# Hybrid encoder layer on one core: gate rows, token rows and Toeplitz blocks issued at other places

## The chip, the cores and the metric

The kernel runs on one core of a Trainium2 chip. Its time is device microseconds (us) from start to end of one execution. TensorE is called PE (its weight loads PEld), VectorE DVE, ScalarE ACT, GpSimd POOL and SyncE SP. SP issues most transfers between the chip's memory (DRAM) and on-chip memory, each by one instruction of its queue. POOL and ACT issue some too.

## What is computed

One layer (`DEPTH = 1`) of a hybrid encoder, in fp32, on a prompt of 2048 rows and 64 sample rows that continue a cached stream of 2048:

```
h = rms(x, ln1);  q, k, v, fg, u, hc, gb, gc = split(h @ w_in)     # 8 heads of 64
logf = log_sigmoid(fg + bf);  c = cumsum(logf)
s = q k^T / 8 + c_q - c_k, causal;  att = softmax(s) v
y_ssm, state = s5(u)            # 16 groups of 16 channels, 64 complex states each
ssm = gelu(y_ssm) * sigmoid(gelu(y_ssm) @ w_glu + b_glu)
conv = gb * shortconv(gc * hc)
x = x + concat(rms(att), rms(ssm), rms(conv)) @ w_out
x = x + relu(rms(x) @ w_up)^2 @ w_down
```

The outputs are the new rows, keys, values, gate logs, S5 states and conv states of both streams.

## The kernel before

`phase1` (to about 542 us) makes the in-projection and leaves queries and keys (`qk_d`), values (`v_d`), token rows of the S5 branch (`u_d`) and gate sums (`nc_d`) in DRAM; its last part is the conv. `attention` (to about 1080 us) goes over the eight prompt heads. Out-projection, up-projection and down-projection follow and are not touched.

For a head `h`, `load(h)` (L1196) brings into one of two sets of tiles: `kb` (keys with three gate rows from `nc_d`, 24 KB, L1200, and 64 key rows, 512 KB, L1201), `q1` (64 transposed query rows, L1202; its three last rows carry maxima, for head 0 from `m_d` by ACT, L1207) and `ka` (keys again, two halves, L1203 and L1204). `load_v` (L1210) brings the values, 1 MB, into `v3`, and `load_q2` (L1215) one block of 512 transposed queries, two transfers of 128 KB (L1220, L1221). In the trace `q1` and `q2` are both called `q`, `v3` is `v`. `scores` runs units of a head in the order of `order()`: two products into `st` (L1239 reads `kb` and `q1`, L1240 `ka` and `q2`), the exponential on ACT (L1248), its split into `ph` and `pl`, and the products with `v` into `po` (L1260, L1262, L1267). Beside them `row_max` (L1149, L1154) takes the maxima of the next head, for which that head's `kb` and `q1` must be there.

Between units `fill(w)` advances a chain of generators by weights that they `yield`: `s5_branch` (L786), in which a `yield -1` hands over to `sample_attention` for four pairs of sample heads, then w_out and the output of the sample rows. `s5_branch` loads its token rows in three chunks of 704 KB (`s5ut`, `load_u`, L808), the first at its start, makes tables, writes kernels to `kp_d`, and loads these as eight Toeplitz blocks of 256 KB (`s5mt`, L922), which `s5py` reads from 944 us on. `sample_attention` loads 512 cached keys at a time (`sa_y`, L1084), transposes them in four products (`sa_pk`, L1081) and makes scores (`sa_ps`, L1090, L1091); a chunk's load overwrites what the transposes before it read.

A scheduler writes each engine's order from the order of the code and its priorities; each engine runs its own order in sequence. A transfer of SP or ACT signals its landing on one of eight semaphores in turn, so it also waits for the transfer eight before it. POOL stores the conv state (L419, L423) and the S5 states (L952) in pieces of four bytes.

Of the kernel before, what the change touches and what calls it, by code (L numbers as in the profile page):

```python
# [48 lines left out]
def f32(ap):  # L49
    return ap.bitcast(F32)  # L50
# [735 lines left out]
def s5_branch(g, pool, sp):  # L786

    nc, I, O = g.nc, g.I, g.O
# [129 lines left out]
        nc.sync.dma_start(hs[hh, 129, :], I[src][0, 0].rearrange("g p -> p g"))  # L918

    mt = pool.tile([128, G, 256], F32, tag="gm", name="s5mt")  # L920
    for t in range(8):
        nc.sync.dma_start(mt[16 * t:16 * t + 16],  # L922
                          g.kp_d[:, :, 16 * (7 - t):16 * (7 - t) + 256].rearrange("g c n -> c g n"))
        yield 1
    r1 = sp.tile([128, 16, G], F32, tag="yg", bufs=3, name="s5r1")
    r2 = sp.tile([128, 16, G], F32, tag="yg", bufs=3, name="s5r2")

# [240 lines left out]
def attention(ctx, g, fill):  # L1168

    tc, nc = g.tc, g.nc  # L1170
# [7 lines left out]
    ka, kb, q1, v3 = [], [], [], []  # L1178
# [17 lines left out]
    def load(h):  # L1196
        i, hp, e = h % 2, h // 2, h % 2
        r = slice(64 * e, 64 * e + 64)
        qk = g.qk_d[hp]
        nc.sync.dma_start(f32(kb[i])[64:67, :], g.nc_d[:, h, :])  # L1200
        nc.sync.dma_start(f32(kb[i])[0:64, :], qk[0, 1, r, :])  # L1201
        nc.sync.dma_start(f32(q1[i])[0:64, :], qk[0, 0, r, :])  # L1202
        nc.sync.dma_start(f32(ka[i])[0:64, :], qk[0, 1, r, :])  # L1203
        nc.sync.dma_start(f32(ka[i])[64:128, :], qk[1, 1, r, :])  # L1204
        if h == 0:
            load_q2(0, 3)
            nc.scalar.dma_start(f32(q1[i])[64:67, :], g.m_d)  # L1207
            load_v(0)

    def load_v(h):  # L1210
        i, hp, e = h % 2, h // 2, h % 2
        nc.sync.dma_start(f32(v3[i])[:, :, 0:128],
                          g.v_d[hp][e])

    def load_q2(h, sb):  # L1215
        hp, e = h // 2, h % 2
        r = slice(64 * e, 64 * e + 64)
        c = slice(sb * 512, sb * 512 + 512)
        t = pp.tile([128, 512], F32R, tag="q2", bufs=3, name=f"q2{h}_{sb}")
        nc.sync.dma_start(f32(t)[0:64, :], g.qk_d[hp][1, 0, r, c])  # L1220
        nc.sync.dma_start(f32(t)[64:128, :], g.qk_d[hp][0, 0, r, c])  # L1221
        q2[h, sb] = t
# [59 lines left out]
    def order():  # L1282
        full = {sb: [(sb, (k, k + 1)) for k in range(0, 4 * sb, 2)] for sb in range(4)}
        diag = {sb: [(sb, (4 * sb,)), (sb, (4 * sb + 1,)), (sb, (4 * sb + 2, 4 * sb + 3))] for sb in range(4)}
        f3, f2, f1 = full[3], full[2], full[1]
        d3, d2, d1, d0 = diag[3], diag[2], diag[1], diag[0]
        u = f3[:2] + [d3[0], f3[2], d0[0], f3[3], d3[1], d0[1], f3[4], d0[2], f3[5], d3[2]]
        u += f2[:2] + [d2[0], f1[0], d1[0], f2[2], d2[1], f1[1], d1[1], f2[3], d1[2], d2[2]]
        seen, out = {}, []
        left = {sb: len(full[sb]) + 3 for sb in range(4)}  # L1290
        for sb, b in u:
            left[sb] -= 1
            w = 2.2 if b[0] < 4 * sb else 1.2
            out.append((sb, b, sb not in seen, left[sb] == 0, w))
            seen[sb] = 1
        return out

    units = order()
    total = sum(u[4] for u in units)
    fill(0.1)  # L1300
    load(0)
    pend, pend2 = [], []

    def late(n, m):
# [8 lines left out]
    for h in range(H):  # L1313
# [9 lines left out]
        for n, (sb, batch, first, last, w) in enumerate(units):  # L1323
            if n == 0 and h + 1 < H:
                load(h + 1)
            if n == 1:
                load_q2(h, 0)
            if n == 3 and h + 1 < H:
                load_v(h + 1)
            if n == 6:  # L1330
                load_q2(h, 2)
            if n == 11:
                load_q2(h, 1)
            if n == len(units) - 4 and h + 1 < H:
                load_q2(h + 1, 3)
            pend.append(scores(h, sb, batch, first, last))
            if n >= 2:
                owed += 43.0 * w / (total * 0.74)
            maxima()
            if len(pend) > 2:  # L1340
                f, f2 = pend.pop(0)
                f()
                pend2.append(f2)
            maxima()
            fill(w)
            if len(pend2) > 1:
                pend2.pop(0)()
            maxima()
            g.late = h + 1 == H and n >= 12
# [12 lines left out]
def w_out_tiles(g, pool, tags, dtype, out):  # L1362
    for tag, n in tags:
        t = pool.tile([128, n, D], dtype, tag=tag, name=f"wo_{tag}{len(out)}")
        out += [t[:, j, :] for j in range(n)]


def w_out_load(g, pool, tags):
    k0 = len(g.wo_r)
    w_out_tiles(g, pool, tags, F32, g.wo_r)  # L1370
    for k in range(k0, len(g.wo_r)):
        g.nc.sync.dma_start(g.wo_r[k], g.I["w_out"][0, k * 128:k * 128 + 128, :])


def w_out_split(g, k):

    nc = g.nc
    raw, hi, lo, w = g.wo_r[k], g.wo_h[k], g.wo_l[k], g.bn[:, k:k + 1]
    nc.scalar.activation(hi, raw, AF.Copy, scale=w)
    nc.vector.scalar_tensor_tensor(lo, raw, w, f32(hi), op0=ALU.mult, op1=ALU.subtract)  # L1380
# [474 lines left out]
@with_exitstack  # L1855
def hybrid_step_kernel(ctx, tc, I, O, dbg=None):
    g = setup(ctx, tc, I, O)
    with ExitStack() as c1:
        phase1(c1, g)
    with ExitStack() as c2:  # L1860
        fpool = c2.enter_context(tc.tile_pool(name="fill", bufs=1, side="right", reuse_waits="tile"))
        fsp = c2.enter_context(tc.tile_pool(name="fills", bufs=1, side="right", reuse_waits="tile"))

        def chain():
            for y in s5_branch(g, fpool, fsp):
                if y < 0:
                    yield from sample_attention(g, fpool, fsp, (0, 1))
                    g.idle = True
                    yield from sample_attention(g, fpool, fsp, (2, 3))
                else:  # L1870
                    yield y

            w_out_load(g, fpool, (("hs", 2), ("ych", 2)))
            w_out_tiles(g, fpool, (("u", 4),), F32R, g.wo_h)
            w_out_tiles(g, fpool, (("x1", 2), ("x2", 2)), F32R, g.wo_l)
            yield 4
            for k in range(4, 8):
                w_out_split(g, k)
                yield 0
            yield from out_sample(g, fpool)  # L1880
            while not g.late:
                yield 0
            g.prep[0] = out_prep(g, 0)
            for _ in range(3):
                next(g.prep[0])
                yield 4

        clock = Ctx()
        clock.now, clock.ready, clock.budget = 0.0, 0.0, 0.0
        it = chain()  # L1890

        def side_by_side(*gens):
            ready = {x: clock.now for x in gens}
            while ready:
                x = min(ready, key=ready.get)
                if ready[x] > clock.now:
                    yield ready[x] - clock.now
                y = next(x, None)
                if y is None:
                    del ready[x]  # L1900
                else:
                    ready[x] = clock.now + y
                    if y == 0:
                        yield 0

        g.side_by_side = side_by_side

        def fill(w):

            clock.now += w * 1.68  # L1910
            clock.budget = min(clock.budget + w, 4.0)
            while clock.budget > 0 and clock.now >= clock.ready:
                y = next(it, None)
                if y is None:
                    break
                clock.ready = max(clock.now + y, clock.ready)
                clock.budget -= 0.4 if y > 0 else 1.25

        g.ah = c2.enter_context(tc.tile_pool(name="ah", bufs=1, reuse_waits="tile"))
        g.os = c2.enter_context(tc.tile_pool(name="os", bufs=2, reuse_waits="tile"))  # L1920
        g.ready, g.prep, g.late, g.idle = {}, {}, False, False
        g.fpool, g.fsp = fpool, fsp
        with ExitStack() as c2a:
            attention(c2a, g, fill)
            for _ in it:
                pass
        with ExitStack() as c3:
            phase3a(c3, g)
    g.wts, g.fts, g.first = {}, {}, {}
    with ExitStack() as c6:  # L1930
        g.xp = c6.enter_context(tc.tile_pool(name="both", bufs=1, reuse_waits="tile"))
        with ExitStack() as c4:
            phase_up(c4, g)
        with ExitStack() as c5:
            phase_down(c5, g)
    if dbg is not None:
        dbg(g)
# [30 lines left out]
```

## Time and profile before

| | |
|---|---|
| time, median of 3 runs | 2792.05 us (2791.56 to 2795.51) |
| the profiled execution's own time | 2794.95 us |
| its span, first to last instruction | 2793.2 us |
| granted TensorE clock, mean | 0.979 |
| busy share of PE, DVE, ACT, POOL | 97%, 60%, 44%, 15% |

The profile is of one execution, and its times are from the start of the span. The granted clock is the share of full speed (2.4 GHz) that PE was given; 0.50 is the lower level, 1.2 GHz. An engine's idle time is put down to what ended it, as inferred from semaphores; "issue" is a time for which the profile shows no releaser.

### The profile page before, as it was taken

Reading aid. Unit: us, or ns where it says so; the run is one execution under the profiler, and the core shown is the slowest. Engines: PE = TensorE matmul, PEld = TensorE weight load, DVE = VectorE, ACT = ScalarE, POOL = GpSimd, SP = SyncE. Lnnn points to the kernel's source line nnn. Section 1 sums busy time; section 2 is a strip of 40 time slices with the busy share of each in tenths; the row PEclk is TensorE's granted clock in tenths of the full one; section 3 lists DMA queues with packets and bytes.
Section 4 is the critical chain, followed back from the end, with each engine's and each line's share of the span. In section 5 each row is a group of like instructions: output and inputs, shape, how many; then the busy total and the mean of one; then the engine's idle time right before and its main releaser. Section 6 shows DMA issues by size and latency. Waiting matters only on the chain.

```text
span 2793.2 us, 38960 instructions
## 1 busy us (share of the span) xinstructions
PE 2699.9 (97%) x14438; PEld 2341.8 (84%) x14438; DVE 1681.7 (60%) x3375; ACT 1230.3 (44%) x2383; POOL 415.4 (15%) x566
## 2 busy tenths in 40 slices
PE   7999999888899999899989999999999999999999
PEld 7999998755567776688789999999998888888887
DVE  7637468477575576577786686686644344434433
ACT  5424243156577677833265676576641111111110
POOL 2101105123752224432300000000000000000000
PEclk9999999989899999999999999999999999999999
DMA  7636546643644223375545353344354122212123
GB/s 216 186 109 185 165 104 177 111 99 93 108 100 109 72 71 89 116 213 165 177 137 176 131 176 127 133 156 136 128 198 151 51 78 80 78 48 78 49 79 117
DMA packets 358929, 347.13 MB, mean 124 GB/s; under 512 B 43726, under 2 KB 316446, under 8 KB 354734
## 3 DMA queue, kind: packets, MB, share of 16 engines
q1 hardware_dynamic: 356189, 336.87, 41.8%
q0 software_dynamic: 2240, 7.01, 0.8%
q8 instruction: 114, 1.87, 0.3%
q14 instruction: 76, 0.62, 0.1%
q10 hardware_dynamic: 310, 0.75, 0.1%
HBM read 237.05 MB, written 107.46 MB: 123 GB/s over the span
## 4 chain that ended last, share of the span: by engine, by line
PE 85%; DMA 4%; issue 4%; DVE 3%; ACT 2%; POOL 1%; SPq 1%; ACTq 0%; DVEq 0%; POOLq 0%
PE pa L1641 12%; PE pd L107 8%; PE pd L108 8%; PE pd L106 8%; PE pd L1641 6%; PE pb L1641 3%; PE pq L106 3%; PE pq L108 3%; PE pq L107 3%; PE mx L1149 2%; PE po L106 2%; PE st L1239 2%; PE po L107 2%; PE po L108 2%; PE st L1240 2%
## 5 line engine op out<-in xcount | busy, mean ns | idle before, releaser
L1820 DVE TENSOR_TENSOR acc<-acc,pd 128x512 f32<-128x512 f32 x272 | 186.7, 686 | 411.2 <-PE pd L108 406.0
L106 PE MATMUL pd<-dw,fh 128*128 128x512 f32 x1016 | 395.2, 389 | 0.0
L108 PE MATMUL pd<-dw,fl 128*128 128x512 f32 x1016 | 395.2, 389 | 0.0
L107 PE MATMUL pd<-dw,fh 128*128 128x512 f32 x1016 | 395.2, 389 | 0.0
L1789 ACT ACTIVATE fh<-fr 128x512 fp32r<-128x512 f32 x127 | 80.2, 632 | 530.9 <-PE pd L107 520.9
L1252 DVE TENSOR_TENSOR pl<-p,ph 128x512 fp32r<-128x512 f32 (+2 forms) x246 | 171.5, 715 | 110.7 <-ACT ph L1251 104.5
L107 PEld LDWEIGHTS pd<-dw,fh 128*128 128x128 f32 x1016 | 190.7, 188 | 39.7
L108 PEld LDWEIGHTS pd<-dw,fl 128*128 128x128 f32 x1016 | 190.7, 188 | 39.6
L106 PEld LDWEIGHTS pd<-dw,fh 128*128 128x128 f32 x1016 | 190.7, 188 | 39.5
L1154 DVE TENSOR_REDUCE pm<-mx 128x1 f32<-128x512 f32 (+2 forms) x320 | 184.3, 607 | 58.7 <-PE mx L1153 32.3
L1248 ACT ACTIVATE p<-st 128x512 f32<-128x512 f32 (+2 forms) x320 | 164.3, 544 | 89.8 <-PE st L1240 34.2
L1641 PE MATMUL pa<-as,wt 128*128 128x352 f32 x1152 | 201.3, 323 | 0.8 <-ACT sm L1656 0.8
L1641 PEld LDWEIGHTS pa<-as,wt 128*128 128x128 f32 x1152 | 187.3, 188 | 2.0 <-ACT sm L1656 1.3
L106 PE MATMUL pq<-wh,xh 128*128 128x384 f32 (+1 forms) x512 | 179.4, 350 | 5.2 <-ACT xh L233 4.7
L1251 ACT ACTIVATE ph<-p 128x512 fp32r<-128x512 f32 (+2 forms) x320 | 173.8, 581 | 3.9 <-PE po L1262 1.8
L108 PE MATMUL pq<-wh,xl 128*128 128x384 f32 (+1 forms) x512 | 174.5, 341 | 0.5 <-DVE xl L234 0.3
L107 PE MATMUL pq<-wl,xh 128*128 128x384 f32 (+1 forms) x512 | 174.1, 340 | 0.0
L1586 DVE TENSOR_TENSOR wt<-tt,wt 128x512 fp32r<-128x512 f32 x192 | 131.4, 687 | 69.1 <-ACT wt L1585 65.9
L1586 DVE TENSOR_TENSOR w<-wr,w 128x512 fp32r<-128x512 f32 x144 | 99.0, 688 | 87.2 <-ACT w L1585 86.9
L1585 ACT ACTIVATE wt<-tt 128x512 fp32r<-128x512 f32 x192 | 120.4, 627 | 67.2 <-PE pd L1641 66.2
L1240 PE MATMUL st<-q,ka 128*128 128x512 f32 (+2 forms) x320 | 124.4, 393 | 12.0 <-DMA q<-qk_d 12.0
L1149 PE MATMUL mx<-kb,q 66*128 66x512 f32 (+2 forms) x280 | 113.4, 438 | 18.1 <-DVE pm L1154 11.1
(508 smaller groups left out, 6118.6 us busy)
## 6 DMA issues: line engine op xcount, KB each, us to landing
wr<-in_w_up_dram SPq DMA_DIRECT2D x46, 1024.0 KB
f_d<-sm SPq DMA_DIRECT2D x47, 704.0 KB
fr<-f_d SPq DMA_DIRECT2D x128, 256.0 KB
raw<-in_w_in_dram SPq DMA_DIRECT2D x51, 512.0 KB
dr<-in_w_down_dram SPq DMA_DIRECT2D x32, 512.0 KB
qk_d<-stgT SPq DMA_DIRECT2D x16, 768.0 KB
xt<-in_x_prompt_dram SPq DMA_DIRECT2D x16, 512.0 KB
ka<-qk_d SPq DMA_DIRECT2D x16, 512.0 KB
```

Of the source, the lines that this page charges most:

```text
L106: nc.tensor.matmul(out, lh, rh, start=first, stop=False)
L107: nc.tensor.matmul(out, lh, rl, start=False, stop=False)
L108: nc.tensor.matmul(out, ll, rh, start=False, stop=last)
L1149: nc.tensor.matmul(p[:, :n], q1[0:66, t * 128:t * 128 + 128], kb[0:66, k0 * 128:k0 * 128 + n], start=True, stop=not last)
L1154: nc.vector.tensor_reduce(pm[:, t, c:c + 1], p[:, :n], axis=AX.X, op=ALU.max)
L1240: nc.tensor.matmul(st[:, c0:], ka[i][:, kc], q2[h, sb][:, c0:512], start=False, stop=r < 0)
L1248: nc.scalar.activation(p[:, c0:], st[:, c0:], AF.Exp)
L1251: nc.scalar.activation(ph[:, c0:], p[:, c0:], AF.Copy)
L1252: (nc.gpsimd if g.idle and j else nc.vector).tensor_tensor(pl[:, c0:], p[:, c0:], f32(ph)[:, c0:], op=ALU.subtract)
L1586: ve.tensor_tensor(t[:, 1], x, f32(t)[:, 0], op=ALU.subtract)):
L1641: nc.tensor.matmul(bank, w[:, x, k], a[:, y, k], start=first and k + j == 0, stop=k + j == 5, skip_group_check=not first)
L1820: nc.vector.tensor_tensor(a[:, o], a[:, o], p, op=ALU.add)
```

## The change

In the first head, the gate rows are issued behind the first block of transposed queries, ahead of the values. `load(0)` stands ahead of `fill(0.1)`, so the first chunk of token rows is issued behind head 0's loads. The eight Toeplitz loads are taken out of `s5_branch`'s sequence into a generator, which runs side by side with the last two pairs of sample heads.

```
--- before.py
+++ after.py
@@ -918,10 +918,14 @@
         nc.sync.dma_start(hs[hh, 129, :], I[src][0, 0].rearrange("g p -> p g"))
 
     mt = pool.tile([128, G, 256], F32, tag="gm", name="s5mt")
-    for t in range(8):
-        nc.sync.dma_start(mt[16 * t:16 * t + 16],
-                          g.kp_d[:, :, 16 * (7 - t):16 * (7 - t) + 256].rearrange("g c n -> c g n"))
-        yield 1
+
+    def toeplitz():
+        for t in range(8):
+            yield 4
+            nc.sync.dma_start(mt[16 * t:16 * t + 16],
+                              g.kp_d[:, :, 16 * (7 - t):16 * (7 - t) + 256].rearrange("g c n -> c g n"))
+
+    g.toeplitz = toeplitz
     r1 = sp.tile([128, 16, G], F32, tag="yg", bufs=3, name="s5r1")
     r2 = sp.tile([128, 16, G], F32, tag="yg", bufs=3, name="s5r2")
 
@@ -1197,13 +1201,15 @@
         i, hp, e = h % 2, h // 2, h % 2
         r = slice(64 * e, 64 * e + 64)
         qk = g.qk_d[hp]
-        nc.sync.dma_start(f32(kb[i])[64:67, :], g.nc_d[:, h, :])
+        if h:
+            nc.sync.dma_start(f32(kb[i])[64:67, :], g.nc_d[:, h, :])
         nc.sync.dma_start(f32(kb[i])[0:64, :], qk[0, 1, r, :])
         nc.sync.dma_start(f32(q1[i])[0:64, :], qk[0, 0, r, :])
         nc.sync.dma_start(f32(ka[i])[0:64, :], qk[0, 1, r, :])
         nc.sync.dma_start(f32(ka[i])[64:128, :], qk[1, 1, r, :])
         if h == 0:
             load_q2(0, 3)
+            nc.sync.dma_start(f32(kb[i])[64:67, :], g.nc_d[:, h, :])
             nc.scalar.dma_start(f32(q1[i])[64:67, :], g.m_d)
             load_v(0)
 
@@ -1297,8 +1303,8 @@
 
     units = order()
     total = sum(u[4] for u in units)
+    load(0)
     fill(0.1)
-    load(0)
     pend, pend2 = [], []
 
     def late(n, m):
@@ -1866,7 +1872,7 @@
                 if y < 0:
                     yield from sample_attention(g, fpool, fsp, (0, 1))
                     g.idle = True
-                    yield from sample_attention(g, fpool, fsp, (2, 3))
+                    yield from side_by_side(sample_attention(g, fpool, fsp, (2, 3)), g.toeplitz())
                 else:
                     yield y
```

In the order of the engines the line numbers of the changed kernel are 3 to 6 higher. SP at the first head before; `kb_6570`, `q_6571`, `ka_6572`, `v_6573` are head 0's tiles, `kb_6577` and `q_6578` head 1's, `q_3` is `q2` of block 3:

```order
L1200 DMA kb_6570<-nc_d 3x2048
L1201 DMA kb_6570<-qk_d_60 64x2048
L808 DMA s5ut_6586<-u_d 88x2048
L1202 DMA q_6571<-qk_d_60 64x2048
L1203 DMA ka_6572<-qk_d_60 64x2048
L1204 DMA ka_6572<-qk_d_60 64x2048
L1220 DMA q_3_6593<-qk_d_60 64x512
L1221 DMA q_3_6593<-qk_d_60 64x512
L1212 DMA v_6573<-v_d_64 128x16x128
L1200 DMA kb_6577<-nc_d 3x2048
L1201 DMA kb_6577<-qk_d_60 64x2048
```

And in the changed kernel:

```order
L1206 DMA kb_6570<-qk_d_60 64x2048
L1207 DMA q_6571<-qk_d_60 64x2048
L1208 DMA ka_6572<-qk_d_60 64x2048
L1209 DMA ka_6572<-qk_d_60 64x2048
L1226 DMA q_3_6585<-qk_d_60 64x512
L1227 DMA q_3_6585<-qk_d_60 64x512
L1212 DMA kb_6570<-nc_d 3x2048
L1218 DMA v_6573<-v_d_64 128x16x128
L808 DMA s5ut_6596<-u_d 88x2048
L1205 DMA kb_6577<-nc_d 3x2048
L1206 DMA kb_6577<-qk_d_60 64x2048
```

The gate rows (`nc_d`) and `s5ut` have left the front; the gate rows stand ahead of `v`, `s5ut` behind it and ahead of head 1's loads. SP at the passage from head 2 to head 3 before; here `kb_6577`, `q_6578` and `ka_6575` are head 3's, `q_0` is `q2` of head 2, block 0:

```order
L922 DMA s5mt<-kp_d 16x16x256 x2
L1164 DMA q_6571<-mt_8117 1x16x128
L922 DMA s5mt<-kp_d 16x16x256 x4
L1200 DMA kb_6577<-nc_d 3x2048
L1201 DMA kb_6577<-qk_d_61 64x2048
L1202 DMA q_6578<-qk_d_61 64x2048
L1203 DMA ka_6575<-qk_d_61 64x2048
L1204 DMA ka_6575<-qk_d_61 64x2048
L922 DMA s5mt<-kp_d 16x16x256
L1220 DMA q_0_8243<-qk_d_61 64x512
L1221 DMA q_0_8243<-qk_d_61 64x512
```

And in the changed kernel:

```order
L1168 DMA q_6571<-mt_8311 1x16x128
L1081 DMA sa_c_8358<-ncs_d 4x1x512
L1088 DMA sa_y_8244<-in_cache_k_dram 128x4x128
L1205 DMA kb_6577<-nc_d 3x2048
L1081 DMA sa_c_8421<-ncs_d 4x1x512
L1088 DMA sa_y_8244<-in_cache_k_dram 128x4x128
L1206 DMA kb_6577<-qk_d_61 64x2048
L1207 DMA q_6578<-qk_d_61 64x2048
L1208 DMA ka_6575<-qk_d_61 64x2048
L1209 DMA ka_6575<-qk_d_61 64x2048
L1226 DMA q_0_8465<-qk_d_61 64x512
L1227 DMA q_0_8465<-qk_d_61 64x512
```

Six of the eight `s5mt` are no longer there (two are ahead of this piece, the others are issued beside later sample loads), and loads of sample keys (`sa_y`) and gate sums (`sa_c`) stand among head 3's loads. PE at the first units of head 2 before:

```order
L1239 MATMUL st_3_0_8218<-q_6571,kb_6570 128x512
L1240 MATMUL st_3_0_8218<-q_3_8120,ka_6572 128x512
L1239 MATMUL st_3_1_8225<-q_6571,kb_6570 128x512
L1240 MATMUL st_3_1_8225<-q_3_8120,ka_6572 128x512
L1239 MATMUL st_3_2_8246<-q_6571,kb_6570 128x512
L1240 MATMUL st_3_2_8246<-q_3_8120,ka_6572 128x512
L1239 MATMUL st_3_3_8253<-q_6571,kb_6570 128x512
L1240 MATMUL st_3_3_8253<-q_3_8120,ka_6572 128x512
```

And in the changed kernel:

```order
L1094 MATMUL sa_ps_8390<-sa_y_8244,qbd 128x512
L1245 MATMUL st_3_0_8436<-q_6571,kb_6570 128x512
L1246 MATMUL st_3_0_8436<-q_3_8314,ka_6572 128x512
L1245 MATMUL st_3_1_8443<-q_6571,kb_6570 128x512
L1246 MATMUL st_3_1_8443<-q_3_8314,ka_6572 128x512
L1095 MATMUL sa_ps_8390<-sa_c_8358,sa_i 128x512
L1245 MATMUL st_3_2_8468<-q_6571,kb_6570 128x512
L1246 MATMUL st_3_2_8468<-q_3_8314,ka_6572 128x512
L1245 MATMUL st_3_3_8475<-q_6571,kb_6570 128x512
L1085 MATMUL sa_pk_8423<-ident,sa_y_8244 128x128 x4
L1246 MATMUL st_3_3_8475<-q_3_8314,ka_6572 128x512
```

The second group of sample scores (`sa_ps`) and the third group of transposes (`sa_pk`) now stand among head 2's first scores, ahead of the first L1153 of head 3; before, the first such group stood behind that product (L1149).

## Rows read from the trace of the kernel before

**Rows 1.** The page: busy us, share of span, instructions.

```profile
PE 2699.9 (97%) x14438; PEld 2341.8 (84%) x14438; DVE 1681.7 (60%) x3375; ACT 1230.3 (44%) x2383; POOL 415.4 (15%) x566
```

**Rows 2.** Waits of PE, 540 to 1080 us: total, times, longest.

```profile
PE st L1240 <- DMA q<-qk_d: 12.0, 2, 11.6
...
PE mx L1149 <- issue: 6.3, 1, 6.3
```

**Rows 3.** Windows: busy per engine (PE first), granted clock, DMA share, GB/s.

```profile
545.00:555.00 10.00, 0.00 (x0) 0.00 (x0) 0.07 (x3) 0.00 (x0) 0.38 (x3) 0.51 0.42 65
555.00:563.00 8.00, 6.77 (x17) 4.24 (x18) 3.46 (x5) 6.36 (x11) 0.00 (x0) 0.55 1.05 239
732.00:739.00 7.00, 0.74 (x3) 0.34 (x2) 0.07 (x1) 0.00 (x0) 6.49 (x10) 0.81 0.98 96
739.00:747.00 8.00, 7.59 (x21) 4.15 (x22) 4.22 (x9) 1.19 (x2) 7.41 (x11) 0.50 1.04 182
747.00:754.00 7.00, 6.29 (x18) 3.89 (x19) 3.75 (x6) 5.66 (x12) 6.41 (x11) 0.54 0.49 132
```

**Rows 4.** Timeline of PE, first head: start, length, what, [idle before <-releaser].

```profile
542.61 0.85 PE L1239 MATMUL st<-q,kb 67*128 67x512 f32 x3
555.07 1.62 PE L1240 MATMUL st<-q,ka 128*128 128x512 f32 x3 [11.61 <-DMA q<-qk_d]
...
559.81 0.67 PE L1260 MATMUL po<-ph,v 128*65 128x512 f32 x1
```

**Rows 5.** Waits of SP, 536 to 562 us.

```profile
SPq L1220 <- DMA m_d<-mt: 16.1, 1, 16.1
...
SPq L1221 <- DMA q<-m_d: 1.6, 1, 1.6
```

**Rows 6.** Timeline of SP, first head: issue start, length, transfer.

```profile
508.85 0.53 SPq L808 DMA_DIRECT2D s5ut<-u_d  x1
...
522.94 0.59 SPq L1204 DMA_DIRECT2D ka<-qk_d  x1
...
542.32 0.60 SPq L1212 DMA_DIRECT2D v<-v_d  x1
543.02 10.52 SPq L1200 DMA_DIRECT2D kb<-nc_d  x1
```

**Rows 7.** Timeline of POOL, first head.

```profile
540.08 0.71 POOL L419 DMA_DIRECT2D out_dram<-z  x1 [6.65 <-DVE zs L401]
```

**Rows 8.** Transfer rate, 500 to 580 us, 40 slices of 2 us.

```profile
GB/s 235 5 0 0 78 217 143 184 86 0 1 66 0 49 25 86 243 257 187 34 78 15 3 6 7 18 143 311 249 218 213 209 219 217 222 386 295 284 161 180
```

**Rows 9.** Timeline of SP, head 2 to head 3.

```profile
715.87 3.47 SPq L922 DMA_DIRECT2D s5mt<-kp_d  x4
...
720.29 0.59 SPq L1202 DMA_DIRECT2D q<-qk_d  x1
```

**Rows 10.** Timeline of PE, head 2 to head 3.

```profile
723.50 0.42 PE L1239 MATMUL st<-q,kb 67*128 67x512 f32 x1
...
738.83 0.55 PE L1149 MATMUL mx<-kb,q 66*128 66x256 f32 x1 [6.26 <-issue]
...
740.32 1.06 PE L1081 MATMUL sa_pk<-ident,sa_y 128*128 128x128 f32 x4
...
742.72 2.08 PE L1090 MATMUL sa_ps<-sa_y,qbd 128*128 128x512 f32 x2
744.73 0.79 PE L1091 MATMUL sa_ps<-sa_c,sa_i 4*128 4x512 f32 x1
...
747.02 0.77 PE L1240 MATMUL st<-q,ka 128*128 128x512 f32 x1 [0.43 <-DMA q<-qk_d]
```

**Rows 11.** Chain, 715 to 748 us: start, length, what.

```profile
727.60 19.29 DMA q<-qk_d
```

**Rows 12.** Timeline of POOL, head 2 to head 3.

```profile
723.29 0.90 POOL L952 DMA_DIRECT2D out_dram<-s5hs  x1
```

**Rows 13.** Transfer rate, 700 to 752 us, 40 slices of 1.3 us.

```profile
GB/s 0 0 0 0 0 0 123 82 8 165 100 121 32 169 69 165 115 113 128 137 187 221 202 202 206 78 19 64 120 158 161 159 145 153 189 258 233 113 11 102
```

More of the change, by code (lines that the diff above doesn't have):

```diff
@@ L920, in s5_branch, with toeplitz @@
     mt = pool.tile([128, G, 256], F32, tag="gm", name="s5mt")
[L921 to L924, printed above, removed]
+    def toeplitz():
+        for t in range(8):
+            yield 4
+            nc.sync.dma_start(mt[16 * t:16 * t + 16],
+                              g.kp_d[:, :, 16 * (7 - t):16 * (7 - t) + 256].rearrange("g c n -> c g n"))
+    g.toeplitz = toeplitz
     r1 = sp.tile([128, 16, G], F32, tag="yg", bufs=3, name="s5r1")
@@ L1199, in load @@
         qk = g.qk_d[hp]
-        nc.sync.dma_start(f32(kb[i])[64:67, :], g.nc_d[:, h, :])
+        if h:
+            nc.sync.dma_start(f32(kb[i])[64:67, :], g.nc_d[:, h, :])
         nc.sync.dma_start(f32(kb[i])[0:64, :], qk[0, 1, r, :])
@@ L1206, in load @@
             load_q2(0, 3)
+            nc.sync.dma_start(f32(kb[i])[64:67, :], g.nc_d[:, h, :])
             nc.scalar.dma_start(f32(q1[i])[64:67, :], g.m_d)
@@ L1299, in attention @@
     total = sum(u[4] for u in units)
+    load(0)
     fill(0.1)
-    load(0)
     pend, pend2 = [], []
@@ L1868, in chain @@
                     g.idle = True
-                    yield from sample_attention(g, fpool, fsp, (2, 3))
+                    yield from side_by_side(sample_attention(g, fpool, fsp, (2, 3)), g.toeplitz())
                 else:
```

## The prediction

> **What bounds the kernel now.** The page comes first: TensorE (PE) is busy for 97% of the span [rows 1]. So the time falls only where PE stands still or runs at the lower of its two clock levels. The waits of PE over the attention phase say where that is: one wait of 11.6 us of L1240 for a `q<-qk_d` load, and one of 6.3 us ahead of L1149, whose releaser the view does not name ("issue") [rows 2]. The windows add the clock. Around the first wait the granted clock is 0.51 and 0.55, around the second 0.81, then 0.50 and 0.54, which is the 1.2 GHz level [rows 3]. Work done in those windows takes twice its time.
>
> **The first head (place A).** PE's timeline: the three L1239 of the first units start at 542.61, L1240 only at 555.07, the first `po` (L1260, which needs the values `v`) at 559.81 [rows 4]. Why `q2` was late stands in SP's waits: L1220 waited 16.1 us for `m_d<-mt`, L1221 then 1.6 us for `q<-m_d` [rows 5]. By the code neither reads those; they are held by the completion semaphores that SP's and ACT's transfers share. After them SP issued `v` at 542.32, then head 1's gate rows, whose issue alone took 10.52 us [rows 6]. Meanwhile almost nothing moved: from 542 to 552 the rate is 15, 3, 6, 7 and 18 GB/s, then 143, 311, 249 [rows 8]. What stands at the start of that hole are POOL's stores of four-byte pieces at 540.08 [rows 7]. The trace shows the coincidence, not the cause.
>
> **The second place (B), head 2 going over to head 3.** SP issued four Toeplitz blocks in a row at 715.87 and head 3's `q` only behind them, at 720.29 [rows 9]. PE reached L1149 at 738.83 - 6.26 = 732.57 and stood for 6.26 us; L1240 waited another 0.43 at 747.02 [rows 10]. The chain of that stretch confirms the transfers: 19.29 us are `q<-qk_d` [rows 11]. In the rate there is a second hole, 78, 19 and 64 GB/s from 732.5 to 736.4, behind POOL's small stores issued at 723.29 [rows 12, 13].
>
> **The change, part by part.** The same bytes move and the same matmuls run. What changes is who stands behind whom.
>
> *Gate rows and `q2` at A.* With `kb<-nc_d` and `s5ut` out of the front, `q2` gets other semaphores and goes right behind `ka`. In the trace `ka` went out at 522.94 [rows 6], so `q2` lands near 541, just ahead of the hole, instead of behind 552. The 11.6 us wait for `q2` is gone. But the three gate rows now stand between `q2` and `v`; my reading of the order is that they, and `v` behind them, inherit the waits for `m_d<-mt` and `q<-m_d`, so `v` goes out about when it did, at 542.3 to 543, into the same hole. What is late next is `v`. From 552 on the bus moved the 256 KB of `q2` and 1 MB of `v`; without the 256 KB, at 249 to 311 GB/s, `v` comes 0.8 to 1.0 us earlier. Against this stands the clock: it stayed low until about 8 us after PE started at 555 [rows 3, 4]; if the real start is now at 559, about 4 us more run at half speed, a loss near 2 us, of which the scores done ahead of `v` give back some. I take 0 for A; the bounds are -3.3 (`v` at 556.5, the hole ending as before and the rate 311) and +4.
>
> A price for the gate rows: the row is the 10.52 us that issuing head 1's took [rows 6]. I take nothing for it, since it lies inside the hole in which `v` can't move either; uncovered it would be up to 10.
>
> The Trainium skill, "DMA: Bandwidth & Descriptors", section "Why a DMA increments its semaphore by 16 and not by 1", speaks against this move: a transfer is dealt over the largest number of engines, up to 16, that divides its slowest dimension, so three rows use three engines. By that rule alone the 24 KB would cost an estimated half microsecond at the rates above, and the sum would be 0.5 us worse; the row's 10.52 us, taken uncovered, would make it 10 worse.
>
> *`s5ut` behind `v`.* The first 704 KB chunk went out at 508.85 with no one waiting [rows 6]. Now it stands ahead of all of head 1's loads: at 213 to 249 GB/s [rows 8] it pushes them by 2.9 to 3.4 us. Those loads had some slack, since PE shows no further wait of that kind in [rows 2]. Bounds 0 and +3.4; I take +1.
>
> *Toeplitz blocks at B.* Six of the eight leave the stretch (1.5 MB, 7.6 us at the 206 GB/s seen there [rows 13]), and parts of the next sample pair take their place. On PE, four groups of `sa_pk` and three of `sa_ps` move ahead of the first L1149. At half clock they took 1.06 us for four transposes and 2.08 + 0.79 for a score group [rows 10]; at full clock half, so 4 x 0.53 + 3 x 1.43 = 6.4 us. These are busy times that overlap; I take 5.5. PE is ready for L1149 at 732.57 + 5.5 = 738.1.
>
> When does `q` come? SP now issues `kb` behind a `sa_y` load that must wait until PE has done the third `sa_pk` group, which stands beside the L1239 of 723.50. With two groups of each kind ahead of it (2 x 0.53 + 2 x 1.43 = 3.9), that is at 727.4, and `q` goes out near 728.7, 8.4 us later than before. Ahead of its last byte are 256 + 512 + 512 KB; at 206 GB/s 6.4 us, so 735; if the hole of three slices (3.9 us) falls into it, 739. The wait is 0 to 1 us. For L1240, `q2` is 1.31 MB further on: 741.5 to 745.5. PE comes there about 4 us after 738.1 (of the 8.2 us between L1149 and L1240, 0.43 were wait and 3.9 sample work; the rest is halved, and 2 us of other items come in). So it waits 0 to 3.5; I take 2, and 1 for a clock that may fall.
>
> What goes: 6.26 + 0.43 of waiting, and half of the 7.59 + 6.29 us of PE work at 0.50 and 0.54 [rows 3], 6.7. Together 13.4; less 3 is 10.4. Bounds of B: 13.4 gained, or nothing.
>
> *The blocks at their new places.* They go out beside later sample loads, far from their reader (`s5py`), in stretches without a wait of PE. Bounds 0 and +2; I take +0.5.
>
> **Sum.** 0 + 1 - 10.4 + 0.5 is about -9, from 2794.95 us of the profiled execution to 2786. That execution is 2.9 us above the median of the runs (2792.05), and the terms are the same for both: I predict **2783 us**. What a measurement of this kernel can tell from no change is about 0.2%, 5.6 us; the border to "faster" is 2786.5.
>
> **The rivals.**
>
> *Both waits go* (0.08). If `v` too lands early, near 548.5, then L1260 starts 11 us earlier than 559.81, and some 2 us of half clock go as well: 2783 - 13 = 2770. For it: SP may pass the gate rows without the 10.52 us. Against: the hole of [rows 8] begins before `v` goes out.
>
> *The wait at B stays* (0.22). If `q` lands 6 us after PE's 738.1, the wait and the cold stretch are as before, and the gain is what little is left, 0 to 5 us: 2787 to 2792. For it: the loads are issued 8 us later than before, behind PE itself.
>
> *Slower by the tie between SP and PE at B* (0.13). Before, `q` took from 720.29 to the end of the wait at 738.83, 18.5 us. If it takes as long from 728.7, it lands at 747.2, PE waits 9 us instead of 6.3, and `q2` behind it, 19.29 us from 731 on, lands at 750, where PE would want L1240 at half clock near 753. That loses some 3 us, and the 3.4 us of `s5ut` come on top: 2792 + 6 = 2798. It decides from 744.4 on: a `q` landing later than that makes the wait longer than the old 6.3 us. Against it: six blocks that filled the queue are no longer ahead.
>
> *The blocks don't move far enough* (0.05): two of eight stay where they were; if the queue was not the cause but POOL's stores, nothing changes: 2792.
>
> The forecast has 0.52, with its own range 2778 to 2788. Reaching to the others until no more than 2 in 10 is left out gives 2775 to 2794. Faster: most of the forecast's 0.52 and the first rival, 0.58; same 0.29; slower 0.13.
>
> **What would show it.** At A: no wait of L1240 (now L1246) for `q`, and in its place a wait of about 10 us of L1260 (now L1266) or of its followers for `v`, with the clock still near 0.5 to 565. At B: the idle time before L1149 (now L1153) under 2 us, the clock 1.00 from 732 to 754, `q` issued near 728.7. Wrong would be: a wait at B of 6 us or more; a new wait of PE over 3 us between 570 and 700 for head 1's loads, or between 760 and 860; or an idle stretch at A longer than the old one.

## The result, and the profile after

The change makes the kernel **slower**: 2809.93 to 2813.24 us in three runs, against 2791.56 to 2795.82 us in four runs of the kernel before; the ratio is 1.0056, 95% interval [1.0043, 1.007]. Forecast were 2783 us and a range from 2775 to 2794. A fourth run of the changed kernel took 3761.5 us at a granted clock of 0.65 and is left out. The profiled execution took 2811.0 us, 16 us more than that of before.

The page's busy row of PE answers to [rows 1]: 4.4 us more work for the same 14438 matmuls, and a smaller share of a longer span.

```profile
PE 2704.3 (96%) x14438; PEld 2343.2 (83%) x14438; DVE 1688.1 (60%) x3370; ACT 1228.5 (44%) x2383; POOL 419.1 (15%) x571
```

The waits of PE from 540 to 600 us (total, times, longest) answer to the first row of [rows 2]:

```profile
PE po L1266 <- DMA v<-v_d: 9.0, 1, 9.0
...
PE st L1245 <- DMA kb<-nc_d: 1.3, 1, 1.3
PE mx L1153 <- DMA q<-qk_d: 1.2, 1, 1.2
```

The 11.6 us wait for `q2` is gone; in its place PE waits 9.0 us for `v`, 1.3 for the gate rows and 1.2 for head 1's `q`, which comes later. From 720 to 800 us:

```profile
PE sa_pk L1085 <- DMA sa_y<-in_cache_k_dram: 15.4, 2, 8.0
PE mx L1153 <- DVE pm L1158: 3.4, 6, 0.8
```

The wait at the maxima (L1149 before, L1153 now) has gone from place B. Two waits for cached keys of the sample heads have come instead, 15.4 us together, where the kernel before had 6.26 and 0.43 [rows 10]. The chain of 720 to 800 us (start, length, what) gives the places, and a stretch behind the first of them in which PE and DVE take turns:

```profile
726.49 11.45 DMA sa_y<-in_cache_k_dram
737.99 1.12 PE sa_pk L1085 x4
...
752.14 0.51 PE mx L1153
752.76 0.70 DVE pm L1158
754.48 0.52 PE mx L1153
755.02 0.70 DVE pm L1158
756.81 0.81 PE mx L1153
...
781.56 11.56 DMA sa_y<-in_cache_k_dram
793.25 1.08 PE sa_pk L1085 x4
```

What stands ahead of both loads is in POOL's timeline and in SP's (issue start, length, transfer); first POOL's two pairs of stores of the S5 states:

```profile
725.03 0.90 POOL L956 DMA_DIRECT2D out_dram<-s5hs  x1
...
726.79 0.84 POOL L957 DMA_DIRECT2D out_dram<-s5hs  x1
```

Then SP's:

```profile
726.49 0.39 SPq L1088 DMA_DIRECT2D sa_y<-in_cache_k_dram  x1
726.93 0.37 SPq L1205 DMA_DIRECT2D kb<-nc_d  x1
...
740.13 0.59 SPq L1207 DMA_DIRECT2D q<-qk_d  x1
...
781.56 0.40 SPq L1075 DMA_DIRECT2D sa_y<-in_cache_k_dram  x1
```

The load of 726.49 feeds the third group of transposes (`sa_pk`), the one at 737.99; the load behind that group goes out at 739.13 and head 3's `q` right after it. Each of the two late loads goes out beside or right behind a pair of stores; the second pair was issued at 779.52 and 781.02. The kernel before had the second pair at the same time (779.42 and 780.92), but its next `sa_y` load only at 789.57, when they were done. The transfer view of 715 to 800 us (40 slices of 2.1 us, then the stores' size and the time from issue to landing) shows how little moved while these loads ran, 1 to 44 GB/s from 728 to 738 us and 8 to 101 from 781 to 793. It also shows what a 4 KB store takes, as the median of the four:

```profile
GB/s 14 123 8 0 0 4 1 41 26 30 44 12 27 265 212 193 212 209 293 293 77 12 0 63 114 14 76 164 10 102 44 43 8 37 37 73 101 325 196 9
...
out_dram<-s5hs POOLq DMA_DIRECT2D x4, 4.0 KB, 10.9
```

The windows (busy and number of matmuls for PE first, then the granted clock, DMA share and GB/s) say what it cost. First the kernel before, then the changed one:

```profile
720.00:740.00 20.00, 13.32 (x63) 8.82 (x61) 8.27 (x10) 8.43 (x17) 18.83 (x24) 0.91 1.07 140
...
780.00:800.00 20.00, 20.00 (x118) 14.54 (x117) 16.75 (x29) 12.62 (x26) 18.75 (x24) 1.00 0.36 84
...
840.00:860.00 20.00, 19.96 (x108) 13.39 (x107) 15.67 (x27) 11.38 (x23) 3.83 (x3) 1.00 0.41 110
```

```profile
720.00:740.00 20.00, 12.51 (x63) 8.66 (x61) 6.80 (x8) 8.90 (x21) 18.61 (x28) 0.80 0.11 16
...
780.00:800.00 20.00, 11.97 (x55) 7.99 (x54) 10.35 (x18) 5.55 (x10) 18.62 (x27) 0.74 0.50 91
...
840.00:860.00 20.00, 17.99 (x84) 11.02 (x83) 10.25 (x18) 13.57 (x29) 3.96 (x3) 1.00 0.65 172
```

From 720 to 740 us the two do the same x63: there a new wait has taken the place of the old one. What puts the changed kernel behind comes later, above all from 780 to 800 us, with x55 against x118.

### The profile page after: what moved, and what is told of

Read it like the earlier page. It is cut to its first block, busy times and chain, and to the rows that moved or that the text cites. A ratio compares the mean times of both kernels' runs of the same rounds, so it can differ in the third digit from the quotient of the medians.

```text
span 2809.0 us, 38939 instructions
## 1 busy us (share of the span) xinstructions
PE 2704.3 (96%) x14438; PEld 2343.2 (83%) x14438; DVE 1688.1 (60%) x3370; ACT 1228.5 (44%) x2383; POOL 419.1 (15%) x571
## 4 chain that ended last, share of the span: by engine, by line
PE 86%; issue 4%; DMA 3%; DVE 3%; ACT 2%; POOL 1%; SPq 1%; ACTq 0%; DVEq 0%; POOLq 0%
PE pa L1647 13%; PE pd L108 8%; PE pd L107 8%; PE pd L106 8%; PE pd L1647 6%; PE pb L1647 3%; PE pq L108 3%; PE pq L106 3%; PE pq L107 3%; PE mx L1153 2%; PE po L106 2%; PE po L108 2%; PE po L107 2%; PE st L1245 2%; PE st L1246 2%
## 5 line engine op out<-in xcount | busy, mean ns | idle before, releaser
L1258 POOL TENSOR_TENSOR pl<-p,ph 128x512 fp32r<-128x512 f32 (+1 forms) x79 | 96.1, 1218 | 267.8 <-ACT ph L1257 199.3
L1266 PE MATMUL po<-ph,v 128*65 128x512 f32 (+2 forms) x320 | 124.2, 393 | 12.0 <-DMA v<-v_d 9.0
```

Source lines behind the costliest of these rows:

```text
L1258: (nc.gpsimd if g.idle and j else nc.vector).tensor_tensor(pl[:, c0:], p[:, c0:], f32(ph)[:, c0:], op=ALU.subtract)
L1266: nc.tensor.matmul(acc[0:65, c0:512], v3[i][:, kt, 64:129], ph[:, c0:], start=first and j == 0, stop=False)
```

## The experiments

Each ratio is to the kernel before, run beside it on the same chip, with its 95% interval; a point is 0.01 of the ratio, 28 us, and 0.1 point is 2.8 us. The runs use these edits, alone or together. **A**: the change's two edits at the first head. **B**: its edit on the Toeplitz blocks. **S** and **Z**: the S5 states and the conv state are transposed on PE and stored as rows instead of four-byte pieces; nothing is left out of the computation. **Q**: the first block of `q2` is issued ahead of the next head's loads.

### The change cut in two

`e1_head_only` is the kernel before with A, `e2_blocks_only` with B; their diffs are parts of the one above.

> Kernel before with the head-0 edits alone (gate rows behind q2, token rows behind the values); the Toeplitz blocks as before. Theory (small stores at the second place): the loss is not here; the wait of 11.6 us for q becomes one of some 9 us for v, head 1's loads come a few us later, time within 5 us of before, about 2794. Rival (the head-0 edits cost the time): 2805 or more.

> Kernel before with the Toeplitz edit alone (blocks in a generator beside the last two pairs of sample heads, which start earlier). Theory: all of the loss is here: PE waits for cached keys (sa_y) of 6 to 9 us at two places, 725 to 800 us, time 2808 to 2816. Rival (head-0 edits): 2792 or less, since the 6.3 us wait at L1149 goes.

Measured: A 1.0018 [1.0009, 1.0026], 2798.9 us, by the ratio 5.0 us slower, at the edge of what its theory allowed. Its profile has `v` late by 10.9 us at the first head, and the old wait at the maxima of place B, now 8.2. B 1.0069 [1.0057, 1.0082], 2815.3 us, with 13.4 us of waits for `sa_y`. So the loss is in the blocks' edit, as the theory had it. The two add up to 0.87 point, more than the 0.56 of both, so they share something.

### The four-byte stores

`e3_after_rows` is the changed kernel with S, `e4_before_rows` the kernel before with S, `e5_before_conv_rows` the kernel before with Z.

```
 S: -        po.dma_start(O[o][0, 0].rearrange("g p -> p g"), hs[lo, j, :])
    -        po.dma_start(O[o + 1][0, 0].rearrange("g p -> p g"), hs[hi, j, :])
    ...
    +        nc.tensor.transpose(p[:16, 0:128], hs[:, j, :], g.ident)
    ...
    +        ac.activation(ht, p[:16, 0:128], AF.Copy)
    +        po.dma_start(O[o][0, 0], ht[:, lo])
    +        po.dma_start(O[o + 1][0, 0], ht[:, hi])
 Z: -            nc.gpsimd.dma_start(O[7][0, 0, :, cs].rearrange("j c -> c j"), z[:, npr:npr + 2])
    ...
    +            nc.tensor.transpose(pz[:2, 0, :], z[:, npr:npr + 2], g.ident)
    ...
    +            nc.scalar.activation(zr[:2], pz[:2], AF.Copy)
    +            nc.gpsimd.dma_start(O[7][0, 0, :, cs], zr[:2, 0, :])
```

(Lines left out are marked by three dots. Z does the same with the store at L423.)

> Changed kernel, but the S5 states are transposed on TensorE (two products) and stored as 16 rows of 256 bytes, after the sample heads, in place of POOL's four-byte stores at 725 and 780 us. Theory (cached-key loads are caught by the four-byte stores): both sa_y waits (15.4 us) go and the clock stays up, 2782 to 2795. Rival (SP issues the cached keys too late because they wait for PE's transposes, and PE for them): the waits stay at 5 us or more, 2805 or more.

> Kernel before with the S5 states transposed and stored as rows after the sample heads, all else as before. Theory, carried back: the 6.3 us wait at L1149 came in good part from the same stores: it falls under 3 us, 2780 to 2788. Rival (the eight Toeplitz blocks ahead in the queue make it, as predicted): the wait stays at 5 us or more, 2789 to 2795.

> Kernel before, with the conv state transposed on TensorE and stored as rows of 512 bytes instead of four-byte pieces (L419, L423); all else as before. Theory (the hole in the rate at the first head is made by these stores): the wait of 11.6 us for q falls under 4 us, the rate after 542 us stays above 100 GB/s, 2778 to 2786. Rival (the hole comes from the loads of head 0 themselves or from SP's slow issue of the gate rows): the wait stays at 9 us or more, 2790 to 2798.

Measured: e3 1.0025 [1.0014, 1.0035], 2801.4 us; e4 0.9968 [0.9957, 0.9978], 2787.7 us; e5 0.9968 [0.9956, 0.9981], 2784.5 us. In e3 the waits of PE from 720 to 800 us are

```profile
PE mx L1157 <- DVE pm L1162: 3.4, 6, 0.8
PE sa_pk L1089 <- DMA sa_y<-in_cache_k_dram: 0.7, 1, 0.7
```

so 15.4 us of waiting became 0.7, and yet e3 is not back at the kernel before. In e4 the 6.3 us became 1.3, with 3.9 for `q2`; its profiled execution took 2796.2 us, 8.5 above its median, so that trace shows the waits but not the gain. In e5 the 11.6 us wait at the first head is gone without a successor; its windows there have x190 matmuls in 40 us, where the kernel before had x112 (x31 and x81):

```profile
540.00:560.00 20.00, 18.43 (x96) 13.31 (x94) 11.59 (x30) 10.47 (x20) 3.51 (x6) 0.91 0.91 227
560.00:580.00 20.00, 19.18 (x94) 13.38 (x95) 12.47 (x23) 13.46 (x31) 0.00 (x0) 0.83 0.68 172
```

What follows: the stores make the waits at both places. At the first head it is their form, since e5 stores the same bytes some 6 us later (546.38 instead of 540.08), beside running loads, and these go on at 182 to 358 GB/s. At B form and place changed together: with S the stores go out only near 938 us, as four stores of 4.0 KB, each in rows of 256 bytes, that land 2.6 us after issue (e3). But S is worth 0.31 point to the changed kernel and 0.32 to the kernel before. The stores explain the waits, and by themselves not the gap between the two kernels.

### The blocks' move without the earlier sample pairs

B takes eight `yield 1` out of `s5_branch`, so the sample pairs start eight slots earlier. `e6_blocks_no_early` is the kernel before with B and these slots put back.

```
     g.toeplitz = toeplitz
+    for t in range(8):
+        yield 1
```

> Kernel before with the Toeplitz blocks taken out of the sequence as in the change, but with eight empty yields of 1 left in their place, so that the sample pairs start where they did before. Theory (the early start of the sample pairs is what costs, not the moved blocks): no wait for sa_y over 1 us, the wait before the first maxima of head 3 under 2 us, 2782 to 2790. Rival (the blocks beside the later sample loads cost): 2800 or more.

Measured: 1.0038 [1.0025, 1.005], 2803.3 us: outside the theory's range and in the rival's. The wait ahead of the first maxima of head 3 is gone, as expected, with POOL's stores where they were (723.26 and 725.27). But PE waits 3.5 us for `q2`, and 2.4 for `sa_y` where at most 1 was expected. From 720 to 760 us e6 does x161 matmuls where the kernel before did x128, so at B the move alone does help. The earlier start costs the 0.31 point between e2 and e6, 8.7 us. But 0.38 stay, and much of it is lost in a place that the waits hardly show: PE's timeline at the passage from head 3 to head 4,

```profile
820.46 0.44 PE L1155 MATMUL mx<-kb,q 66*128 66x384 f32 x1
821.35 0.39 PE L1155 MATMUL mx<-kb,q 66*128 66x256 f32 x1 [0.46 <-DVE pm L1160]
...
823.61 0.39 PE L1155 MATMUL mx<-kb,q 66*128 66x256 f32 x1 [0.78 <-DVE pm L1160]
...
824.59 0.51 PE L1155 MATMUL mx<-kb,q 66*128 66x512 f32 x1 [0.52 <-DVE pm L1160]
825.88 0.69 PE L1155 MATMUL mx<-kb,q 66*128 66x384 f32 x1 [0.78 <-DVE pm L1160]
```

and the window, the kernel before and then e6:

```profile
820.00:840.00 20.00, 20.00 (x113) 14.38 (x112) 12.12 (x25) 16.83 (x35) 2.15 (x2) 1.00 0.31 87
```

```profile
820.00:840.00 20.00, 16.73 (x57) 9.99 (x58) 10.88 (x21) 9.51 (x22) 0.00 (x0) 0.74 0.38 104
```

In PE's order the maxima of the next head stand there in one row from `mx_0_0` to `mx_7_0`, with two sample scores between them, ahead of the first product that needs `q2`; before, that product stands earlier and scores stand between the maxima. From e6:

```
4164 L1155 MATMUL mx_5_1_9434<-kb_6570,q_6571 128x256
...
4167 L1155 MATMUL mx_6_0_9442<-kb_6570,q_6571 128x512
4168 L1155 MATMUL mx_6_1_9458<-kb_6570,q_6571 128x384
...
4171 L1155 MATMUL mx_7_0_9465<-kb_6570,q_6571 128x512
4172 L1246 MATMUL st_0_0_9382<-q_0_9272,ka_6575 128x512
```

Each maximum needs DVE to have emptied a buffer, so PE does one and waits some 0.5 to 0.8 us. From 822 to 826 us it is busy for 1.84 us at a granted clock of 0.87, and from 826 to 835 the clock is 0.50, the lower level. The changed kernel has the same turn-taking at 752 to 760 us, in the chain above, with 0.50 from 756 to 764.

### The queries first

`e10_blocks_q_first` is e6 with Q; `e16_after_s5rows_q_first` is e3 with Q, `e17_before_s5rows_q_first` is e4 with Q.

```
         for n, (sb, batch, first, last, w) in enumerate(units):
+            if n == 0:
+                load_q2(h, 0)
             if n == 0 and h + 1 < H:
                 load(h + 1)
-            if n == 1:
-                load_q2(h, 0)
```

> Kernel before with the blocks moved but the sample pairs not earlier (which took some 8 us more than before), and load_q2(h, 0) issued ahead of load(h + 1) instead of behind it. In PE's order the unbroken rows of maxima at heads 3 and 4, behind the first half of a score, are then broken up by scores. Theory (these rows of PE and DVE in turn, with half clock behind them, are the loss that the list of waits doesn't show): 10 to 18 us less, 2784 to 2793. Rival (the order is a bystander, and the block loads or sample loads cost): 2799 or more.

> The changed kernel with the S5 states stored as rows (as e3_after_rows, 1.0025) and the transposed queries' first block issued ahead of the next head's loads; the convolution's state is still stored in elements. Theory: what e3_after_rows still lacked is the order with long rows of maxima; issuing the queries first takes them away: ratio 0.996 to 0.999, 2782 to 2790 us. Rival: the order is not the cause, what is left is the first head's: 1.001 to 1.003, 2797 to 2802 us.

> The kernel before with the S5 states stored as rows and the transposed queries' first block issued ahead of the next head's loads: the counterpart of e16_after_s5rows_q_first (0.9982), which is the changed kernel with the same two edits. Theory: these two edits give the kernel before about as much as they give the changed one, so what sets the two apart is the change itself in any setting, and this run reads 0.993 to 0.995, 2775 to 2781 us. Rival: stores and order are what makes the change slow, and without them the two kernels meet: this run reads 0.997 or more, 2786 us or more.

Measured: e10 1.002 [1.001, 1.0029], 2801.0 us, in the rival's range; e16 0.9982 [0.9972, 0.9991], 2787.9 us; e17 0.995 [0.9938, 0.9963], 2779.9 us. In e10 a load of cached keys, issued at 781.96 behind one of 1 MB, has moved right behind the element stores again (778.82 and 780.34). The wait of PE for it, out of the waits from 720 to 800 us:

```profile
PE sa_pk L1087 <- DMA sa_y<-in_cache_k_dram: 11.5, 1, 11.5
```

In e16 the stores are out of the way and the edit does what it should: 0.43 point against e3, intervals apart. The windows of 740 to 760 us, e3 and then e16:

```profile
740.00:760.00 20.00, 16.36 (x54) 9.07 (x53) 11.03 (x17) 6.78 (x15) 18.16 (x33) 0.76 0.61 143
```

```profile
740.00:760.00 20.00, 19.36 (x103) 13.17 (x101) 16.50 (x28) 12.91 (x29) 18.24 (x31) 1.00 0.48 121
```

So Q takes away the row of maxima at B, and time with it; how much of the 0.43 is that row's is not shown, since Q also changes when `q2` comes at the other heads. And e17 came in where the theory put it: Q gives the kernel before 0.18 point too, and the gap between e16 and e17 is still 0.32.

### The change on cleared ground

With S and Z in both, `e8_before_both_rows` is the kernel before, `e9_rows_head` adds A, `e7_all` adds A and B with the eight slots kept, `e18_after_both_rows` is the whole change. With Q as well, `e11_rows_q_first` is the kernel before, `e15_rows_blocks_q_first` has the blocks moved with the slots kept, and `e12_after_rows_q_first` is the whole change.

> The head-0 edits, the moved blocks without the early start, and both states (S5 and conv) stored as rows. Theory: all three waits (first head, head 3's maxima, cached keys) are small, 2768 to 2780. Rival (the head-0 edits cost some 4 us on their own, whatever the stores): slower than the same kernel without them, 2780 or more.

> Kernel before with both states stored as rows and nothing else. Theory: the two savings add (9 us of the S5 states, 10 to 14 of the conv state), 2768 to 2778. Rival (the wait passes on to the next load): less than half of the second, 2782 or more.

> Kernel before with both states stored as rows, and the head-0 edits on top. Theory (without the small stores there is nothing left at the first head for these edits to save, and token rows ahead of head 1's loads make those late): 2 to 6 us slower than the same kernel without the edits, 2778 to 2783 where that had 2776. Rival (the edits help once the hole is gone): 2774 or less.

> The changed kernel with both states stored as rows, in the old order of the queries: the counterpart of e8_before_both_rows (0.9938). Theory: the gap between the two kernels stays where it was, at 0.4 to 0.6 points, so this run reads 0.998 to 1.000, 2789 to 2795 us. Rival: the small stores made the gap, and without all of them it is gone or halved: at most 0.9965, 2785 us or less.

> Kernel before with both states stored as rows and load_q2(h, 0) ahead of load(h + 1). Theory: the 3.6 us wait for q and the row of maxima of head 3 go too, another 5 to 10 us: 2766 to 2772. Rival: no less than 2774.

> The changed kernel with both states as rows and load_q2(h, 0) ahead of load(h + 1): the two causes named for its loss taken away, its own edits kept. Theory (small stores and rows of maxima are the whole loss): no wait for cached keys over 1 us, no long row of maxima, 2766 to 2778. Rival (the early sample pairs cost by themselves, as stalls between PE and ACT in the sample heads): 2785 or more.

> The best version so far, e11_rows_q_first (both states stored as rows, the transposed queries' first block issued ahead of the next head's loads, 0.9903), and the Toeplitz blocks moved beside later sample heads without the earlier start of the sample pairs; the first head's edits are left out. Theory: with the stores and the rows of maxima both gone, moving the blocks is worth little, as the 6.3 us wait before was not theirs: 0.989 to 0.992, 2763 to 2772 us. Rival: the blocks do stand in a row's way, and moving them gives 8 us more: at most 0.988, 2762 us or less.

| run | what it has | median us | ratio, 95% interval |
|---|---|---|---|
| e8 | S, Z | 2776.4 | 0.9938 [0.9925, 0.9952] |
| e9 | S, Z, A | 2780.8 | 0.9948 [0.9932, 0.9963] |
| e7 | S, Z, A, B with the slots kept | 2788.5 | 0.9972 [0.9961, 0.9983] |
| e18 | S, Z, A, B | 2787.3 | 0.9976 [0.9966, 0.9986] |
| e11 | S, Z, Q | 2768.1 | 0.9903 [0.9886, 0.9919] |
| e15 | S, Z, Q, B with the slots kept | 2774.2 | 0.993 [0.9918, 0.9942] |
| e12 | S, Z, Q, A, B | 2777.4 | 0.994 [0.9924, 0.9956] |

e8, e9, e11 and e12 came in where their theories had them. For e12 that is the number alone: its theory was that stores and rows of maxima are the whole loss, and yet it is 0.37 point behind e11, which lacks only the change. e7, 12 us above e8, doesn't bear out that the moved blocks help once the waits are gone; it is in its rival's range, but the head's edits that the rival blamed make up only 0.10 of its 0.34 point. e18 lies between its two expectations. e15 lies outside both: no one had expected the moved blocks to cost 0.27 point where nothing is left for them to collide with. The gap of the whole change is 0.56 as it stands, 0.57 with S (e3, e4), 0.32 with S and Q (e16, e17), 0.38 with S and Z (e18, e8) and 0.37 with all three (e12, e11); each is known to some 0.2. So a third or so of the loss seems to go when, beside the S5 stores, either the conv stores or the order of the queries is mended too: three settings agree on it, though no one of them is clear of its error by much. The rest, 9 to 11 us, is the change itself. By the ratios of the first four rows of the table it falls into 0.10 for A, 0.24 for the moved blocks, and 0.04 for the earlier start, which had cost 0.31 beside the small stores; of the three only the 0.24 is clear of its error.

Where e15 loses is read from its trace. From 700 to 800 us it does no fewer matmuls than e11 (x512 against x500); it loses most from 860 to 870 us. The windows of e15, then e11:

```profile
860.00:870.00 10.00, 6.43 (x38) 5.62 (x38) 1.85 (x7) 4.91 (x8) 0.00 (x0) 0.66 0.88 191
```

```profile
860.00:870.00 10.00, 9.96 (x64) 7.94 (x63) 2.38 (x5) 6.40 (x15) 3.32 (x4) 1.00 0.98 206
```

e15's waits of PE from 800 to 880 us name the sample heads' softmax, a chain of DVE and ACT steps beside which PE has nothing to do there (0.6 us of waiting in e11):

```profile
PE sa_pp L1121 <- ACT sa_s L1113: 4.1, 2, 2.8
```

The same wait comes to 3.9 to 4.8 us from 700 to 900 us in each of the four kernels that have Q and the moved blocks (e10, e12, e15, e16) and to 0.6 in the two with Q alone (e11, e17). So it goes with the moved blocks; why they leave the chain without cover is argued, and no run isolates it.

### Which edit of the first head

`e13_rows_tokens` is e8 with `load(0)` ahead of `fill(0.1)`, `e14_rows_gates` e8 with the gate rows moved.

> The kernel before with both states stored as rows, and of the two edits of the first head only the one on the token rows (the branch's token rows are issued behind the values, so ahead of the second head's loads); the gate rows stay where they were. Theory: the some 4 us that the two edits cost together in e9_rows_head (ratio 0.9948 against 0.9938 of e8_before_both_rows) come from the token rows, whose third issue takes some 6 us on SP ahead of the second head's loads: ratio about 0.995, some 2780 us. Rival: they come from the gate rows, and this run reads as e8_before_both_rows, 0.993 to 0.994, some 2775 us.

> The kernel before with both states stored as rows, and of the two edits of the first head only the one on the gate rows (issued behind the transposed queries); the token rows stay where they were. Theory: reads as e8_before_both_rows, ratio 0.993 to 0.994, some 2775 us. Rival: the gate rows are what costs, and this run reads about 0.995, some 2780 us.

Measured: e13 0.9946 [0.9933, 0.9958], 2778.6 us; e14 0.9935 [0.9922, 0.9947], 2775.7 us. Both medians lie where the theory (the token rows cost) puts them, but the intervals overlap each other and that of e8, so it isn't decided.

## Why the prediction was wrong

**The first head (A).** The mechanism was right: `q2` comes in time, `v` inherits its place and PE waits for it, 9.0 us where about 10 was named. The sum was too kind: 0, and +1 for `s5ut`, against +5.0 us for the two edits in e1 (0.18 point) and about 3 on cleared ground (e9 against e8, not clear of the error). Both are inside the bounds given. The coincidence noted at the first head, the hole in the rate behind POOL's stores [rows 7, 8], is the cause there, as e5 shows.

**What made the wait at B.** The term of -10.4 us took the four Toeplitz blocks ahead of head 3's `q` [rows 9] for the cause of the wait, and POOL's stores [rows 12] for a second thing that hits a little later. With the blocks left where they were and only the stores changed, e4 cuts the 6.3 us to 1.3 (3.9 for `q2` come after it). With the stores left and only the blocks moved, e6 has no such wait either. So it takes both to make the wait, and either one's going ends it: the blocks were named rightly, but not alone. The last rival, with 0.05, had named the stores.

**The step that failed** is "When does `q` come?". It let PE be done with its third `sa_pk` group at 727.4 by adding up PE's own work ahead of it, so that the `sa_y` load behind that group, `kb` and `q` could go out by 728.7. The load that feeds the third group was put at nothing. It went out only behind the second group, at 726.49, and took 11.45 us beside the stores of 725.03 and 726.79. PE, which runs its order in sequence, stood 7.35 us at the third group, until 737.99, before it ever came to the maxima. The next `sa_y` load went out at 739.13 and `q` at 740.13, not 728.7. So the 6.26 us went and 7.35 came, and the gain of 10.4 at B did not: from 720 to 760 us the changed kernel does x124 matmuls, the kernel before x128. In e3, without stores nearby, the load that feeds the third group goes out at 729.63 and PE is at the group at 733.62, 4.0 us later.

**The blocks' new places** were put at +0.5 with bounds 0 and +2, for stretches without a wait of PE. This is the second term that failed, and it is where the loss against the kernel before arises. It looked at the blocks and not at what their leaving moves: the sample pairs, a second `sa_y` load of which met the second pair of stores at 781.56 (8.03 us), and the order of PE at the passages from head to head. The blocks' edit as a whole was forecast at -9.9 us and measured at +19 (e2): 8.7 of it the earlier start beside the small stores (e2 against e6), the other 10.6 the move itself (e6), of which 0.24 to 0.27 point, some 7 us, are left on cleared ground.

**The rivals.** The side came out as "slower by the tie between SP and PE" had it, but through `sa_y`, not `q`, and at 16 us, not 6. Two of the signs that the prediction named for being wrong came: a wait at B of 6 us or more (7.35, at the transposes and not at L1153), and a new wait over 3 us between 760 and 860 (8.03, ending at 793.25).

**The gate rows.** Issued at 540.31, they ended a wait of PE of 1.3 us at 544.32. On cleared ground e14 against e8 prices their move at -0.03 point, with an error of some 0.2: the 10 us of the uncovered row, 0.36 point, are not there. Of the Trainium skill's rule that three rows use three engines ("DMA: Bandwidth & Descriptors", section "Why a DMA increments its semaphore by 16 and not by 1") no run here shows the engines, and the half microsecond estimated by it is too small to be seen.

## What to carry to other kernels

Before moving a transfer, look for small-piece stores near its new issue time and near that of everything that moves along with it; if a load that an in-order engine needs lands there, change the stores first. Removing steps from a planned sequence moves the whole plan: compare the engine order at the next few passages, and look for rows of one kind of instruction that wait on one other engine. Count matmuls per window beside the busy share, since such a row shows only small waits and a busy PE. And to tell whether a nuisance explains a gap, take it out of both kernels: the S5 stores cost each of them 0.3 point, so by themselves they are not what sets the two apart.

## What the runs showed of the hardware

A store of 4.0 KB in four-byte pieces took 10.9 us from issue to landing (the median of four in the changed kernel; in the kernel before 15.7 at B, and 8.9 for the second pair, with almost nothing moving beside it). The same 4.0 KB in rows took 2.6 us (e3, near 938 us, with little beside it). While such a store ran, a load of 256 KB from another engine's queue took 11.5 us, about 23 GB/s, with the transfer engines shown busy for 0.11 of the window of 720 to 740 us; in e3, with no such store near, the load was in use 4.0 us after its issue. What holds the load is not shown. The Trainium skill, "DMA: Bandwidth & Descriptors", section "Rules for kernel authors", says that a transfer whose last dimension isn't contiguous becomes one descriptor per element and should be rearranged, and section "Issuing engines are not separate DMA queues" that transfers of all engines interleave on the same 16 DMA engines. The 10.9 us against 2.6 fit the first, but the number of descriptors is not shown: the transfer views count 32 packets per 4.0 KB store in either form. The load of SP's queue that is slow beside a store of POOL's fits the second. The conv state's rows still took 9.3 us to land (e5; 8.7 and 9.8 as elements), but the loads beside them went on at 182 to 358 GB/s: the landing time of a small store doesn't tell what it does to others.

The best version found is e11, the kernel before with both states stored as rows and the queries first: 2768.1 us, 0.9903 [0.9886, 0.9919], against 1.0056 of the change.
